# Compressed-branch probabilities transposed in blocks of 32 rows, with high and low parts stacked for one product, and a longer order search

## The chip, the cores and the metric

The kernel runs on one core of one Trainium2 chip. The metric is the time of one execution on the device in microseconds; of several runs the median is given. The engines are named as the profile names them: PE is TensorE (matmuls; PEld is its loading of weights), DVE is VectorE, ACT is ScalarE, POOL is GpSimd, SP is SyncE, which here only issues transfers.

## The reference

One decoder layer over 512 tokens of width 1024, batch 1, in float32. A single RMS norm feeds one input projection, whose columns go to two groups of eight heads of 64:

```
h = rms_norm(x);  proj = h @ w_in
group A:  o = g0 * o_cmp + g1 * o_sel + g2 * o_win      (gates: sigmoids per head)
group B:  per query the 128 keys with the best indexer score, then softmax attention
out = x + concat(A * silu(z_A), B * silu(z_B)) @ w_out
```

The change lies in the compressed branch, `o_cmp`. The keys and values of 32 neighbouring positions, at a stride of 16, are compressed by a small two-layer network to one key and one value, 31 in all (the kernel pads them to 32). Each query attends to the compressed positions that end at or before it:

```
s = q . kc * 64**-0.5;   p = masked_softmax(s, 16*c + 31 <= t);   o_cmp = p @ vc
```

Eight query heads share two groups of keys and values, four heads to a group.

## The kernel before

TensorE multiplies in a rounded float32 format (`fp32r`). To keep precision, nearly every operand is split into a high part, the rounded value, and a low part, the rest; a projection is then three products (high x high, high x low, low x high).

*Stages.* The indexer's columns are projected while the input arrives; then the chunks C (raw compressed keys and values) and B (other keys and values), the indexer's scores and top-128 selection, the hidden layers of the two compressing networks (`hidden`, `hidden1`, `hidden2`, `hidden3`), the queries (chunks Q1, Q2, D), and then attention, woven with the projections D and Z and, from about 226 us, with the output projection.

*Units of attention.* A unit is one query tile of 128 tokens (`i`, 0 to 3), one group (`g`) and one branch. Units of kind "n" are group A: `b` is 0 for the compressed, 1 for the selected, 2 for the window branch. Units of kind "d" are group B. The 512 rows of a tile and group (128 queries x 4 heads) are handled as four blocks of 128 partitions. `softmax_steps` makes the scores, VectorE adds the mask and ScalarE the exponential (`softmax_of`). `transposed` turns the probabilities by TensorE, so that keys lie on partitions and the 512 rows along the free axis, and splits them into `pth` (high) and `ptl` (low). `times_values` multiplies both by the values: the stationary operand holds the values' high part in 64 columns and their low part in 64 more, and the moving operand is 512 columns wide.

*The compressed unit.* A compressed unit has four blocks of 128x32 probabilities, which lie side by side. They are transposed in one go (line 1045), so that block `h` lands on partitions 32h to 32h+31. For one 512-column product each block needs its own columns, so VectorE copies the result four times through a mask, `diag`, which is one only where row block and column block agree (line 1047, tile `pd`); ScalarE copies that to `ph` (line 1049), and GpSimd makes the rest `pl` (line 1050). Two products of 128 rows and 512 columns follow (line 1068). The values must therefore stand four times over on 128 partitions: `hidden1` copies `uT` with `rep = 4`, and `hidden2` loads it as 128 columns of weights (line 816) and writes 128 rows.

*What sets the order.* `set_order` writes the order on every engine, the transfer queue included. It prices every instruction with `cost`, takes the true dependencies and the rings of buffers, and simulates a backward and a forward pass in turn, `ROUNDS` times; the order whose simulated end is earliest is fixed by dependencies between neighbours on an engine. A matmul is priced by its columns and at least 108 ns.

*Other places that the change touches.* `rope` turns queries and keys with two VectorE products into ring buffers (`RTN` of them, lines 539 and 544) and a GpSimd add (line 545). `tables` fills a pair of rotation tables per kind of head. `ARENA` is the size of a shared memory area.

Of the kernel before, what the change touches and what calls it, by code (L numbers as in the profile page):

```python
# [9 lines left out]
F32 = mybir.dt.float32  # L10
F32R = mybir.dt.float32r
BF16 = mybir.dt.bfloat16
I32 = mybir.dt.int32
AF = mybir.ActivationFunctionType
ALU = mybir.AluOpType

S, D, HD = 512, 1024, 64
NT = S // 128
# [41 lines left out]
C_TOT = C_CSIN + HD  # L60


ARENA = 3689 + 272 - 192
ARENA_R = 5376 - 1024

WARM = 10
RTN, RTX = 8, 1
PD = 3

COST = 1 / 2400  # L70
TBUFS, AHEAD, LAG = 2, 2, 2
# [15 lines left out]

URGENT, SOON = 2000, 300
PE_URGENT, PE_SOON = 200, 60
ROUNDS = 8  # L90

FOUR = {"C": range(4), "B": range(4)}

# [16 lines left out]
def set_order(tc):  # L110
# [18 lines left out]
    def cost(i, e):  # L129

        acc = aps(i)
        n = max(free(ap) for _, ap in acc)
        ins = [ap for w, ap in acc if not w]
        bank = any("PSUM" in str(ap.bass_ap.tensor.space) for ap in ins if hasattr(ap.bass_ap.tensor, "space"))
        if "DMA" in type(i).__name__:
            return 450, 128 * n * 4 / 360
        if e == "PE":
            wide = len(ins) > 1 and str(ins[0].dtype).endswith("float32") and not i.is_transpose

            slow = 2 if str(ins[0].dtype).endswith("bfloat16") else 1  # L140
            return max(108, slow * n * (4 if wide else 1) * 0.432 + 10), 0
        if e == "Activation":
            return (50 if bank else 93) + 0.834 * n + 93 * (len(ins) - 1) + 93 * (len(list(i.outs)) - 1), 0
        small = sum(free(ap) == 1 for ap in ins)
        if e == "DVE":
            if "Max" in type(i).__name__ or "MatchReplace" in type(i).__name__:
                return 69 + 1.041 * n + (62 if "Replace" in type(i).__name__ else 0), 0
            return 69 + 61 * small + (0.521 if len(ins) - small < 2 and not bank else 1.041) * n, 0
        return 161 + 83 * small + (0.834 if len(ins) - small < 2 else 2.06) * n, 0
# [27 lines left out]
    for k, i in enumerate(insts):  # L177
        acc = []
        for w, ap in aps(i):
# [4 lines left out]
            end = off + sum((n - 1) * st for st, n in dims[1:] if st > 0) + 1  # L184
# [125 lines left out]
def tile_hybrid_layer(ctx, tc, xT, x, ng, win, gains, peT, w1, b1, w2, wout, cst, out):  # L310
# [19 lines left out]
    def carve(shape, dt):  # L330

        n = 1
        for d in shape:
            n *= d
        w = n // 2 if dt == BF16 else n
        a = arenas[F32R if dt == F32R else F32]
        v = a[0][:, a[1]:a[1] + w]
        a[1] += w
        if dt == BF16:
            v = v.bitcast(dt)  # L340
        if len(shape) == 1:
            return v
        names = "abcde"[:len(shape)]
        return v.rearrange("p (" + " ".join(names) + ") -> p " + " ".join(names), **dict(zip(names[:-1], shape[:-1])))
# [175 lines left out]

    def tables(j, name):
        gn = gns[:, j, None, :]
        tab = work.tile([128, 2, NT, HD], F32, tag=f"tab{j}", name=f"tab{j}", bufs=1)
        c, s = tab[:, 0], tab[:, 1]
        nc.gpsimd.tensor_tensor(c, cosd, gn[:, :, :HD].to_broadcast([128, NT, HD]), op=ALU.mult)
        nc.gpsimd.tensor_tensor(s, sind, gn[:, :, HD:].to_broadcast([128, NT, HD]), op=ALU.mult)
        return c, s
# [203 lines left out]
    kn = [b8.tile([128, 2, 2 * S + 32], F32R, tag=f"kn{g}", name=f"kn{g}") for g in range(2)]  # L731

    K_CMP, K_SEL = S, S + 32
    diag = carve([4, 128], BF16)
    nc.gpsimd.memset(diag, 0.0)
    for h in range(4):
        nc.gpsimd.memset(diag[32 * h:32 * h + 32, h], 1.0)
    w1t = {}
    FSs = {}

# [57 lines left out]
    def hidden1(kv):  # L798
        hid, u = FSs[kv]
        for half in range(2):  # L800
            nc.tensor.transpose(hid[:, 256 + 64 * half:320 + 64 * half], u[:, 128 * half:128 * half + 128], ident[:64, :64])
        src_ = hid[:, 256:384].rearrange("p (a g c) -> p a g c", a=2, g=2)
        rep = 4 if kv else 1
        uT = work.tile([128, 512], F32, tag="uT", name="uT", bufs=1)[:, :128 * rep]
        uT = uT.rearrange("p (a g r c) -> p a g r c", a=2, g=2, r=rep)
        for half in range(2):
            nc.scalar.copy(uT[:, half], src_[:, half, :, None, :].to_broadcast([128, 2, rep, 32]))
        FSs[kv] = (hid, uT)
        yield 0.2

    def hidden2(kv):
        hid, uT = FSs[kv]
        if kv:
            for g in range(2):
                for half in range(2):
                    nc.tensor.matmul(hid[:, 384 + 64 * g:448 + 64 * g], uT[:, half, g].rearrange("p r c -> p (r c)"),
                                     w2t[:, kv, half], start=(half == 0), stop=(half == 1))
        else:
            c2 = hid[:64, 384:448]
            for half in range(2):  # L820
                nc.tensor.matmul(c2, uT[:, half].rearrange("p g r c -> p (g r c)"), w2t[:, kv, half],
                                 start=(half == 0), stop=(half == 1))
        yield 0.4
        if kv == 0:
            kscr = work.tile([128, 512], F32, tag="t2k", name="kscr", bufs=2)[:64]
            sq = kscr[:, 64:128]
            ss = work.tile([64, 1], F32, tag="kss", name="kss", bufs=1)
            y = work.tile([64, 1], F32, tag="ky", name="ky", bufs=1)
            nc.scalar.activation(sq, c2, AF.Square, scale=0.5, accum_out=ss)
            nc.gpsimd.tensor_scalar(ss, ss, 1.0 / HD, EPS, op0=ALU.mult, op1=ALU.add)  # L830
            rsqrt(y, ss, 1, p=64, tag="nk", magic=MAGIC - 2.0 ** 31)
            cg = kscr[:, 128:256].rearrange("p (a b) -> p a b", a=2)
            nc.gpsimd.tensor_tensor(cg[:, 0], ccos, gkc[:64, 0, :HD], op=ALU.mult)
            nc.gpsimd.tensor_tensor(cg[:, 1], csin, gkc[:64, 0, HD:], op=ALU.mult)
            kr = kscr[:, 256:320].rearrange("p (a b) -> p a b", a=1)
            rope(kr, c2, 1, cg[:, 0:1], cg[:, 1:2], p=64, tag="rk", wide=1)
            kr = kscr[:, 256:320]
            nc.gpsimd.tensor_scalar(kr, kr, y[:, 0:1], 0.5, op0=ALU.mult, op1=ALU.mult)
            FSs["kr"] = kr
        else:  # L840
            for g in range(2):
                c2 = hid[:, 384 + 64 * g:448 + 64 * g]
                nc.scalar.activation(vcs[:, g, 0], c2, AF.Copy, scale=0.5)
                nc.vector.scalar_tensor_tensor(vcs[:, g, 1], c2, 0.5, vcs[:, g, 0].bitcast(F32),
                                               op0=ALU.mult, op1=ALU.subtract)

    def hidden3():
# [190 lines left out]
    def transposed(u, item, parts):  # L1038

        p = ps("T", "T_" + u.name)  # L1040
        ph = work.tile([128, 512], F32R, tag="pth", name="pth", bufs=TBUFS)
        pl = work.tile([128, 512], F32R, tag="ptl", name="ptl", bufs=TBUFS)
        if u.b == 0 and u.kind == "n":

            nc.tensor.transpose(p[:, :128], u.P.rearrange("p h c -> p (h c)"), ident)
            pd = work.tile([128, 4, 128], F32, tag="t2k", name="pd", bufs=2)
            nc.vector.tensor_tensor(pd, p[:, None, :128].to_broadcast([128, 4, 128]), diag, op=ALU.mult)
            pd = pd.rearrange("p h q -> p (h q)")
            nc.scalar.copy(ph, pd)
            nc.gpsimd.tensor_tensor(pl, pd, ph.bitcast(F32), op=ALU.subtract)  # L1050
        else:
            blocks = item[0]
            for b, c in blocks:
                nc.tensor.transpose(p[:, b * 128:(b + 1) * 128], u.P[:, b, c:c + 128], ident)  # L1054
            cols = slice(128 * blocks[0][0], 512)
            nc.scalar.copy(ph[:, cols], p[:, cols])  # L1056
            nc.vector.tensor_tensor(pl[:, cols], p[:, cols], ph[:, cols].bitcast(F32), op=ALU.subtract)  # L1057
        parts.append((u, item, ph, pl))

    def times_values(u, item, *parts):  # L1060
        first = u.o[0] is None
        if first:
            u.o[0] = ps("O", "o" + u.name)
        o = u.o[0]
        end = u.last and item is u.items[-1]
        for cols, v in item[1]:
            for x, pp in enumerate(parts):
                nc.tensor.matmul(o[:, cols], v, pp[:, cols], start=(first and x == 0), stop=(end and x == 1))  # L1068
        if end:
            if u.dst is None:  # L1070
                u.dst = work.tile([128, 2, 128], F32, tag="od_" + u.name, name="od_" + u.name, bufs=1)
                od[u.name[1:3]] = u.dst
            combine(o, u.dst)
            u.done()
        return end
# [372 lines left out]
```

## Time and profile before

| what | value |
|---|---|
| median of 3 runs | 308.2 us (308.15 to 308.23) |
| profiled execution, its span | 306.4 us |
| its granted TensorE clock, mean | 0.999 |
| PE busy | 301.3 us, 98% |
| DVE, ACT, POOL busy | 261.0, 240.7, 235.4 us |
| TensorE's share of the chain that ended last | 86% |
| single transposes of compressed units (line 1045) | 8 |

The span runs from the first to the last instruction of the profiled execution; the time of a run is about 1.8 us longer. Matmuls are pipelined: a recorded length holds the way through the array too, so two in a row overlap, and busy shares of TensorE are read with care. Lines are `line engine operation output<-inputs`, then shapes and counts.

### The profile page before, as it was taken

Reading aid. Unit: us, or ns where it says so; the run is one execution under the profiler, and the core shown is the slowest. Engines: PE = TensorE matmul, PEld = TensorE weight load, DVE = VectorE, ACT = ScalarE, POOL = GpSimd, SP = SyncE. Lnnn points to the kernel's source line nnn. Section 1 sums busy time; section 2 is a strip of 40 time slices with the busy share of each in tenths; the row PEclk is TensorE's granted clock in tenths of the full one; section 3 lists DMA queues with packets and bytes.
Section 4 is the critical chain, followed back from the end, with each engine's and each line's share of the span. In section 5 each row is a group of like instructions: output and inputs, shape, how many; then the busy total and the mean of one; then the engine's idle time right before and its main releaser. Section 6 shows DMA issues by size and latency. Waiting matters only on the chain.

```text
span 306.4 us, 5994 instructions
## 1 busy us (share of the span) xinstructions
PE 301.3 (98%) x1669; PEld 256.4 (84%) x1669; DVE 261.0 (85%) x797; ACT 240.7 (79%) x802; POOL 235.4 (77%) x418
## 2 busy tenths in 40 slices
PE   8999999999999999999999999999999999999995
PEld 5997788899878878888888888888888888888885
DVE  4999699999979998998999999999769989986502
ACT  6965776798969999999989999774379998996400
POOL 3099899997996599987989879985667997686410
PEclk9999999999999999999999999999999999999999
DMA  7995345375410034310121023450443343003011
GB/s 282 415 356 181 96 147 163 92 187 158 114 28 0 0 79 125 106 57 3 38 68 39 3 72 106 136 165 0 141 125 120 106 141 103 4 14 122 20 50 68
DMA packets 21249, 32.42 MB, mean 106 GB/s; under 512 B 5664, under 2 KB 8480, under 8 KB 21216
## 3 DMA queue, kind: packets, MB, share of 16 engines
q1 hardware_dynamic: 21216, 32.05, 34.2%
q8 instruction: 13, 0.21, 0.3%
q14 instruction: 20, 0.16, 0.2%
HBM read 29.04 MB, written 2.47 MB: 103 GB/s over the span
## 4 chain that ended last, share of the span: by engine, by line
PE 86%; DVE 4%; ACT 4%; POOL 3%; DMA 2%; issue 1%; DVEq 0%; POOLq 0%
PE out L1268 15%; PE z L401 14%; PE Q L391 8%; PE D L391 7%; PE B L391 7%; PE on L1068 7%; PE s_n L1033 6%; PE T_n L1054 5%; PE od L1068 3%; PE T_d L1054 3%; PE s_d L1033 3%; PE C L401 2%; PE hid L787 2%; ACT hThi L467 2%; POOL wlo_Q L358 2%; PE idx L699 1%
## 5 line engine op out<-in xcount | busy, mean ns | idle before, releaser
L1010 ACT ACTIVATE P_n<-P_n,arena 128x416 f32<-128x416 f32 (+15 forms) x64 | 33.7, 528 | 4.7 <-DVE arena L1003 4.1
L1003 DVE CUSTOM_DVE_ANT_0 P_n<-s_n,arena 128x416 f32<-128x416 f32 (+15 forms) x64 | 31.0, 499 | 1.0 <-PE s_n L1033 0.4
L1023 POOL TENSOR_SCALAR P_n<-P_n,arena 128x416 f32<-128x416 f32 (+15 forms) x64 | 30.8, 501 | 1.2
L1057 DVE TENSOR_TENSOR ptl<-T_n,pth 128x512 fp32r<-128x512 f32 (+1 forms) x40 | 25.0, 627 | 3.6 <-ACT pth L1056 2.9
L1033 PE MATMUL s_n<-kn,arena_r 128*128 128x512 f32 (+11 forms) x104 | 27.1, 342 | 0.0
L710 DVE MAX8 m<-scores 128x8 f32<-128x512 f32 (+2 forms) x48 | 26.5, 552 | 0.6
L401 PE MATMUL z<-hThi,whi_Z 128*128 128x512 f32 x64 | 26.1, 408 | 0.0
L711 DVE MATCH_REPLACE8 scores<-m,scores 128x512 f32<-128x512 f32 (+2 forms) x48 | 26.0, 542 | 0.1
L401 PE MATMUL z<-hTlo,whi_Z 128*128 128x512 f32 x64 | 25.3, 396 | 0.0
L401 PE MATMUL z<-hThi,wlo_Z 128*128 128x512 f32 x64 | 25.2, 397 | 0.0
L1054 PE MATMUL T_n<-arena,P_n 128*128 128x128 f32 x144 | 24.1, 273 | 0.0
L1268 PE MATMUL out<-whi_wo,mx 128*128 128x512 f32 (+1 forms) x72 | 23.8, 374 | 0.0
L1268 PE MATMUL out<-wohi,mx 128*128 128x512 f32 (+1 forms) x72 | 23.7, 377 | 0.0
L1056 ACT CAST pth<-T_n 128x512 fp32r<-128x512 f32 (+1 forms) x40 | 21.5, 540 | 2.7 <-PE od L1068 1.6
L391 PE MATMUL Q<-whi_Q,hThi 128*128 128x256 f32 (+1 forms) x64 | 22.2, 347 | 0.6 <-DVE kn L587 0.6
L391 PE MATMUL Q<-wlo_Q,hThi 128*128 128x256 f32 (+1 forms) x64 | 21.9, 343 | 0.0
L391 PE MATMUL Q<-whi_Q,hTlo 128*128 128x256 f32 (+1 forms) x64 | 21.9, 344 | 0.0
L1054 PEld LDWEIGHTS T_n<-arena,P_n 128*128 128x128 f32 x144 | 18.1, 140 | 4.0
L1033 PEld LDWEIGHTS s_n<-kn,arena_r 128*128 128x128 f32 x104 | 18.1, 189 | 3.3 <-issue 0.2
L358 POOL TENSOR_TENSOR wlo_Z<-raw_Z,whi_Z 128x512 fp32r<-128x512 f32 x16 | 20.4, 1291 | 0.5 <-ACT whi_Z L357 0.5
L358 POOL TENSOR_TENSOR w1l<-raw_w,w1h 128x512 fp32r<-128x512 f32 x16 | 20.4, 1292 | 0.0
L1068 PE MATMUL on<-pth,arena_r 128*128 128x512 f32 (+1 forms) x48 | 18.3, 382 | 0.0
(270 smaller groups left out, 1108.1 us busy)
## 6 DMA issues: line engine op xcount, KB each, us to landing
raw_w<-in_w_dram SPq DMA_DIRECT2D x16, 256.0 KB, 3.7
raw_Z<-in_win_dram SPq DMA_DIRECT2D x16, 256.0 KB, 2.8
wor<-in_wout_dram SPq DMA_DIRECT2D x16, 256.0 KB, 2.8
raw_Q<-in_win_dram SPq DMA_DIRECT2D x12, 256.0 KB, 3.0
raw_D<-in_win_dram SPq DMA_DIRECT2D x8, 256.0 KB, 2.9
xres<-in_x_dram SPq DMA_DIRECT2D x8, 256.0 KB, 3.0
out_dram<-xres SPq DMA_DIRECT2D x7, 256.0 KB, 2.0
xw<-in_xT_dram SPq DMA_DIRECT2D x2, 860.0 KB, 7.8
```

Of the source, the lines that this page charges most:

```text
L358: engine.tensor_tensor(lo, raw, hi.bitcast(F32), op=ALU.subtract)
L391: nc.tensor.matmul(out_ps, a[:, k, tsl], b, start=(k == 0 and b is hi and a is hT["hi"]), stop=(k == KB - 1 and a is hT["lo"]))
L401: nc.tensor.matmul(out_ps, b[:, csl], a[:, k, :], start=(k == 0 and b is hi and a is hT["hi"]), stop=(k == KB - 1 and b is lo))
L710: nc.vector.max(m8, sc)
L711: nc.vector.match_replace(sc, m8, sc, -3e30)
L1003: nc.vector.tensor_tensor_reduce(P, src_, mask, u.r[:, b:b + 1], 3e38, op0=ALU.add, op1=ALU.min, accum_out=m[:, b:b + 1])
L1010: nc.scalar.activation(P, P, AF.Exp, bias=m[:, b:b + 1], scale=-1.0, accum_out=l[:, b:b + 1])
L1023: nc.gpsimd.tensor_scalar(Pb, Pb, l[:, bb:bb + 1], 1.0 if u.gate is not None else 0.5, op0=ALU.mult, op1=ALU.mult)
L1033: nc.tensor.matmul(p, q[0][:, b], k[:, x], start=(x == 0), stop=(x == 1))
L1054: nc.tensor.transpose(p[:, b * 128:(b + 1) * 128], u.P[:, b, c:c + 128], ident)
L1068: nc.tensor.matmul(o[:, cols], v, pp[:, cols], start=(first and x == 0), stop=(end and x == 1))
L1268: nc.tensor.matmul(p, a, b[:, csl], start=(k == 0 and b is hi and a is mx[0]), stop=(k == 7 and a is mx[1]))
```

## The change

In `transposed`, a compressed unit's four blocks are transposed one by one, each into 32 rows and its own 128 columns. ScalarE copies the result to rows 0 to 31 of `ph`, VectorE writes the rest (result minus high part) to rows 32 to 63 of the same tile, and one product with 64 rows replaces two with 128. The mask `diag` and the tile `pl` fall away for these units, and the values stand twice over on 64 partitions (`rep = 2`), once for each part. `times_values` takes a list of products. Beside that, the prices of matmuls in `cost` are rewritten, `ROUNDS` goes from 8 to 20, the rope ring from 8 buffers to 6, two tables share the buffers of two earlier ones, and `ARENA` is 256 words smaller.

```diff
-ARENA = 3689 + 272 - 192
+ARENA = 3689 + 272 - 192 - 256
-RTN, RTX = 8, 1
+RTN, RTX = 6, 1
-ROUNDS = 8
+ROUNDS = 20
...
         if e == "PE":
-            wide = len(ins) > 1 and str(ins[0].dtype).endswith("float32") and not i.is_transpose
-
+            load = 0.845 * free(ins[1])
+            if i.is_transpose:
+                return max(28, load), 0
+            if str(ins[0].dtype).endswith("float32"):
+                return 2 * max(4 + load, 0.864 * n + 10), 0
             slow = 2 if str(ins[0].dtype).endswith("bfloat16") else 1
-            return max(108, slow * n * (4 if wide else 1) * 0.432 + 10), 0
+            return max(load, slow * n * 0.432 + 10), 0
...
-        tab = work.tile([128, 2, NT, HD], F32, tag=f"tab{j}", name=f"tab{j}", bufs=1)
+        tab = work.tile([128, 2, NT, HD], F32, tag=f"tab{j if j < 3 else 5 - j}", name=f"tab{j}", bufs=1)
...
-    diag = carve([4, 128], BF16)
-    nc.gpsimd.memset(diag, 0.0)
-    for h in range(4):
-        nc.gpsimd.memset(diag[32 * h:32 * h + 32, h], 1.0)
...
-        rep = 4 if kv else 1
-        uT = work.tile([128, 512], F32, tag="uT", name="uT", bufs=1)[:, :128 * rep]
+        rep = 2 if kv else 1
+        uT = work.tile([128, 256], F32, tag="uT", name="uT", bufs=1)[:, :128 * rep]
...
-                    nc.tensor.matmul(hid[:, 384 + 64 * g:448 + 64 * g], uT[:, half, g].rearrange("p r c -> p (r c)"),
+                    nc.tensor.matmul(hid[:64, 384 + 64 * g:448 + 64 * g], uT[:, half, g].rearrange("p r c -> p (r c)"),
                                      w2t[:, kv, half], start=(half == 0), stop=(half == 1))
...
-                c2 = hid[:, 384 + 64 * g:448 + 64 * g]
-                nc.scalar.activation(vcs[:, g, 0], c2, AF.Copy, scale=0.5)
-                nc.vector.scalar_tensor_tensor(vcs[:, g, 1], c2, 0.5, vcs[:, g, 0].bitcast(F32),
+                c2 = hid[:64, 384 + 64 * g:448 + 64 * g]
+                nc.scalar.activation(vcs[:64, g, 0], c2, AF.Copy, scale=0.5)
+                nc.vector.scalar_tensor_tensor(vcs[:64, g, 1], c2, 0.5, vcs[:64, g, 0].bitcast(F32),
                                                op0=ALU.mult, op1=ALU.subtract)
...
         ph = work.tile([128, 512], F32R, tag="pth", name="pth", bufs=TBUFS)
+        if u.b == 0 and u.kind == "n":
+
+            for b in range(4):
+                nc.tensor.transpose(p[:32, b * 128:(b + 1) * 128], u.P[:, b], ident)
+            nc.scalar.copy(ph[:32], p[:32])
+            nc.vector.tensor_tensor(ph[32:64], p[:32], ph[:32].bitcast(F32), op=ALU.subtract)
+            parts.append((u, item, [(cols, v[:64], [ph[:64, cols]]) for cols, v in item[1]]))
+            return
         pl = work.tile([128, 512], F32R, tag="ptl", name="ptl", bufs=TBUFS)
-        if u.b == 0 and u.kind == "n":
-
-            nc.tensor.transpose(p[:, :128], u.P.rearrange("p h c -> p (h c)"), ident)
-            pd = work.tile([128, 4, 128], F32, tag="t2k", name="pd", bufs=2)
-            nc.vector.tensor_tensor(pd, p[:, None, :128].to_broadcast([128, 4, 128]), diag, op=ALU.mult)
-            pd = pd.rearrange("p h q -> p (h q)")
-            nc.scalar.copy(ph, pd)
-            nc.gpsimd.tensor_tensor(pl, pd, ph.bitcast(F32), op=ALU.subtract)
...
-        for cols, v in item[1]:
-            for x, pp in enumerate(parts):
-                nc.tensor.matmul(o[:, cols], v, pp[:, cols], start=(first and x == 0), stop=(end and x == 1))
+        for cols, v, moving in products:
+            done = end and (first or v is products[-1][1])
+            for x, pp in enumerate(moving):
+                nc.tensor.matmul(o[:, cols], v, pp, start=(first and x == 0), stop=(done and x == len(moving) - 1))
```

More of the change, by code (lines that the diff above doesn't have):

```diff
@@ L1041, in transposed, with times_values @@
         ph = work.tile([128, 512], F32R, tag="pth", name="pth", bufs=TBUFS)
-        pl = work.tile([128, 512], F32R, tag="ptl", name="ptl", bufs=TBUFS)
-        if u.b == 0 and u.kind == "n":
-            nc.tensor.transpose(p[:, :128], u.P.rearrange("p h c -> p (h c)"), ident)
-            pd = work.tile([128, 4, 128], F32, tag="t2k", name="pd", bufs=2)
-            nc.vector.tensor_tensor(pd, p[:, None, :128].to_broadcast([128, 4, 128]), diag, op=ALU.mult)
-            pd = pd.rearrange("p h q -> p (h q)")
[L1049 to L1060, printed above, removed]
+        if u.b == 0 and u.kind == "n":
[5 more added lines that the diff above has]
+            return
+        pl = work.tile([128, 512], F32R, tag="ptl", name="ptl", bufs=TBUFS)
+        blocks = item[0]
+        for b, c in blocks:
+            nc.tensor.transpose(p[:, b * 128:(b + 1) * 128], u.P[:, b, c:c + 128], ident)
+        cols = slice(128 * blocks[0][0], 512)
+        nc.scalar.copy(ph[:, cols], p[:, cols])
+        nc.vector.tensor_tensor(pl[:, cols], p[:, cols], ph[:, cols].bitcast(F32), op=ALU.subtract)
+        parts.append((u, item, [(cols, v, [ph[:, cols], pl[:, cols]]) for cols, v in item[1]]))
+    def times_values(u, item, products):
         first = u.o[0] is None
```

## The prediction

> **What bounds the kernel now.** I read the page first: its engine shares, its slices and its chain of waits.
>
> ```profile
> span 306.4 us, 5994 instructions
> PE 301.3 (98%) x1669; PEld 256.4 (84%) x1669; DVE 261.0 (85%) x797; ACT 240.7 (79%) x802; POOL 235.4 (77%) x418
> ...
> PE   8999999999999999999999999999999999999995
> ...
> PEclk9999999999999999999999999999999999999999
> ...
> PE 86%; DVE 4%; ACT 4%; POOL 3%; DMA 2%; issue 1%; DVEq 0%; POOLq 0%
> ```
>
> TensorE is busy in every slice, its clock is fully granted, and 86% of the chain is its work. But a matmul's length in the profile holds a pipeline tail, so I checked two more views: the busy time by stretch, and whom TensorE waited for.
>
> ```profile
> 116.00:156.00 40.00, 40.00 (x223) 34.09 (x221) 37.26 (x135) 37.42 (x175) 36.05 (x83) 1.00 0.24 65
> ...
> 226.00:287.00 61.00, 61.00 (x357) 52.27 (x356) 52.27 (x180) 53.73 (x176) 47.17 (x80) 1.00 0.29 90
> ```
> ```profile
> PE I L444 <- DVE arena L446: 1.2, 1, 1.2
> PE Q L391 <- DVE kn L587: 0.6, 1, 0.6
> ```
> ```profile
> PEld on L1068 <- ACT pth L1056: 0.3, 1, 0.3
> ...
> PEld on L1068 <- POOL ptl L1050: 0.2, 1, 0.2
> ```
>
> From 116 to 287 us, where attention runs, the first column after the stretch (its length) and the next (TensorE) are equal. TensorE waits 1.2 us before its first instruction and 0.6 us once near 92 us, and its weight loads wait 0.3 and 0.2 us in front of value products. So the other engines hide behind TensorE, and the change is worth what it takes from or adds to TensorE's own stream, plus what a new order does to these few waits.
>
> **The price of one instruction in that stream** is the distance from one start to the next, not the length.
>
> ```profile
> 134.43 0.40 PE L391 MATMUL D<-wlo_D,hThi 128*128 128x512 f32 x1
> 134.66 0.39 PE L391 MATMUL D<-whi_D,hTlo 128*128 128x512 f32 x1
> 134.89 0.38 PE L621 MATMUL qT_ps<-arena,R_q 128*128 128x128 f32 x2
> 135.11 0.27 PE L1045 MATMUL T_n<-arena 128*128 128x128 f32 x1
> 135.13 0.47 PE L391 MATMUL D<-whi_D,hThi 128*128 128x512 f32 x1
> 135.45 0.39 PE L391 MATMUL D<-wlo_D,hThi 128*128 128x512 f32 x1
> ```
>
> A 512-column product costs 134.66 - 134.43 = 0.23 us. Two transposes take 135.11 - 134.89 = 0.22, 0.11 each. The compressed unit's single transpose (line 1045) and the product after it take 135.45 - 135.11 = 0.34, so it too costs 0.34 - 0.23 = 0.11.
>
> **What sets a transpose's 0.11 us** decides this case. Either it is the load of its weights, the data: then 32 columns in place of 128 make it cheaper. Or it is the stream of the 128 identity columns: then they do not. I look at two places where the loads were not done ahead, and at the same line's first transposes in windows that end one instruction later each time.
>
> ```profile
> 25.51 0.13 PEld L555 LDWEIGHTS rrow_ps<-arena 128*128 128x128 f32 x1 [0.49 <-DVE arena L435]
> 25.51 0.32 PE L555 MATMUL rrow_ps<-arena 128*128 128x128 f32 x1
> ...
> 25.51 0.19 PEld L555 LDWEIGHTS rrow_ps<-arena 128*128 128x128 f32 x2 [0.49 <-DVE arena L435]
> ...
> 25.51 0.30 PEld L555 LDWEIGHTS rrow_ps<-arena 128*128 128x128 f32 x3 [0.49 <-DVE arena L435]
> 25.51 0.43 PE L555 MATMUL rrow_ps<-arena 128*128 128x128 f32 x2
> ```
> ```profile
> L555 PE MATMUL rrow_ps<-arena x4: 270/272/324, 25.5 to 25.9; 128*128 128x128 f32 x4
> ```
> ```profile
> L801 PEld LDWEIGHTS hid<-arena,scr x4: 135/136/139, 69.2 to 110.7; 64*128 64x128 f32 x4
> L801 PE MATMUL hid<-arena,scr x4: 222/247/272, 69.3 to 110.7; 64*128 64x64 f32 x4
> ```
> ```profile
> 69.25 0.20 PEld L801 LDWEIGHTS hid<-arena,scr 64*128 64x128 f32 x2
> ...
> 69.25 0.33 PE L801 MATMUL hid<-arena,scr 64*128 64x64 f32 x2
> ```
>
> The first transpose of line 555 is recorded with its load at 25.51 and is 324 ns long where the others have 272: it waited 0.05 us for 128 columns of weights. The second load begins 0.19 - 0.13 = 0.06 after the first, which says the same; the third only 0.30 - 0.19 = 0.11 later, because it waits for a transpose to stream. So a load of 128 columns takes 0.06 and the transpose 0.11: the load is not what it waits for. Line 801 loads 64x128, its data, and streams 64x64, the identity: the data are the weights, 128 columns of them again, but only 64 identity columns pass. Its second load begins 0.20 - 0.14 = 0.06 after the first; its second transpose ends at 69.58 and is 0.22 long, so it starts 0.05 after the first had its weights. Half the identity columns, half the price. In the change the identity stays 128x128, so I take **0.11 us for each 32-column transpose too**.
>
> No row has a transpose with 32 columns of weights, so both ends stay open. Below: matmuls that are plain float32 do get cheaper with fewer weight columns.
>
> ```profile
> 117.87 1.00 PE L816 MATMUL hid<-arena,uT 128*128 128x64 f32 x8
> ```
> ```profile
> L816 PE MATMUL hid<-arena,uT x8: 218/275/276, 117.9 to 118.6; 128*128 128x64 f32 x8
> ...
> L821 PE MATMUL hid<-arena,uT x4: 220/222/271, 71.1 to 71.4; 128*64 128x64 f32 x4
> ```
> ```profile
> 71.13 0.45 PE L821 MATMUL hid<-arena,uT 128*64 128x64 f32 x4
> ```
>
> Line 816's eight passes load 128 columns each. The first is the short one, 0.22 long, and the last ends 1.00 after its start, so the ends lie (1.00 - 0.22)/7 = 0.11 apart. Line 821's four passes with 64 columns, the first the long one: (0.45 - 0.27)/3 = 0.06. Halved again, 0.03 is the lower end. It is also the distance at which a product is recorded behind a transpose (135.13 - 135.11 = 0.02). Above: if transposes into 32 rows left the quick form, they would run as plain float32, in two passes, 0.22 us each.
>
> **The change part by part.** *Compressed units, eight of them (x8 in line 1045).* Each loses one 512-column product: 8 x 0.23 = 1.84 us off. Each gains three transposes: 24 x 0.11 = 2.64 us on (ends 24 x 0.03 = 0.72; or 32 x 0.22 - 8 x 0.11 = 6.16). The product that stays has half the rows and all 512 columns: no less.
>
> *The value hidden layer (line 816)* loads 64 columns of weights in place of 128, the form of line 821. Seven distances fall from 0.11 to 0.06: 0.35 us off.
>
> *Other engines.*
>
> ```profile
> L1047 DVE TENSOR_TENSOR pd<-T_n,arena x8: 628/686/694, 117.7 to 271.9; 128x512 f32<-128x512 f32 x8
> L1049 ACT CAST pth<-pd x8: 607/622/627, 119.7 to 272.7; 128x512 fp32r<-128x512 f32 x8
> L1050 POOL TENSOR_TENSOR ptl<-pd,pth x8: 1282/1291/1302, 120.7 to 274.2; 128x512 fp32r<-128x512 f32 x8
> ```
> ```profile
> DVE ptl L1057 <- ACT pth L1056: 7.0, 12, 2.0
> ```
> ```profile
> L1057 DVE TENSOR_TENSOR ptl<-T_n,pth x40: 393/684/693, 104.3 to 280.2; 128x512 fp32r<-128x512 f32 x32, 128x256 fp32r<-128x256 f32 x8
> ```
>
> VectorE loses eight masks of 0.69 and gains eight subtractions of the form of line 1057, 0.69 too: nothing. ScalarE keeps its copy. GpSimd loses 8 x 1.29 = 10.3 us, and a unit's way from transpose to product loses that step. The subtraction waits on VectorE for ScalarE's copy, as line 1057 does: 7.0/12 = 0.6 us a wait, so eight more are 4.7 us. Behind it in VectorE's queue stand the masked softmax sums, for which ScalarE's exponentials wait. All of it lies under TensorE, which is full there; were that cover gone, a unit would cost those 0.6. TensorE waited for line 1050 once, 0.2 us: that is the most the shorter way can bring, and I take 0. The mask's memsets and the halved copies of `uT` lie under it as well; were the cover gone, they would be gains.
>
> *Rings and shared tables.* Six rope buffers for eight make a rope's product on VectorE wait for GpSimd's add of six ropes before. A shared table waits for the ropes of chunk B's keys, which end before the later chunks that fill it. Cost 0, with the rival below.
>
> *The order.* New prices and twenty rounds give another order on every engine. A transpose priced at 28 ns moves no wait if it takes 110: copies and everything queued behind it on TensorE slip by the same amount. What an order can give is the 0.6 and 0.5 us of waits above; what it can cost is a wait like the one at 92 us. I take 0.
>
> **Sum:** 2.64 - 1.84 - 0.35 = +0.45 us on the span of 306.4, so 306.8. The runs' median of 308.2 lies 1.8 above that span; with it, **308.6 us**, between 306.4 + 1.8 - 1.5 = 306.7 (0.72 - 1.84 - 0.35 = -1.47) and, with all 32 in the slow form, 312.2 (6.16 - 1.84 - 0.35 = +3.97).
>
> The Trainium skill, TensorE: Matmul & The Clock Gate, section "LDWEIGHTS (loading the stationary operand)", speaks against my step: load time goes with columns, P/1.2, about 107 ns for 128 and 27 for 32, which would make the 0.11 a load. By that and its section "Back-to-back issue gap" (N/2.4 + 2.5, 56 ns for the 128 identity columns) three more transposes are an estimated 0.17 us a unit, and the kernel would take about 307.3. Here the transposing load took 0.06 for 128 columns, and the measurement decides.
>
> **The rivals.**
>
> *Cheap transposes: the load does set the price.* Line 816 against 821 speaks for it, lines 555 and 801 against. 24 x 0.03: **306.7**. Chance 0.19.
>
> *The order recovers the waits.* TensorE's 0.6 us near 92 us and the two in front of value products go: 308.6 - 1.1 = **307.5**. For it: twenty rounds keep the best of more orders by the plan's reckoning, and GpSimd is freer. Against: the stretches after 116 us show TensorE full already. Chance 0.15.
>
> *Slower: the rope ring holds VectorE before the keys.* In the place where TensorE waited for `kn`, VectorE does rope products and GpSimd is far behind with its adds.
>
> ```profile
> 89.97 0.27 DVE L544 TENSOR_TENSOR rt<-Q,tab 128x128 f32<-128x128 f32 x1
> 90.27 0.69 DVE L587 TENSOR_TENSOR kn<-kT_ps,kn 64x512 fp32r<-64x512 f32 x1
> ```
> ```profile
> 88.08 5.02 POOL L358 TENSOR_TENSOR w1l<-raw_w,w1h 128x512 fp32r<-128x512 f32 x4
> 93.07 2.13 POOL L545 TENSOR_TENSOR R_q<-rt,rt 128x256 f32<-128x256 f32 x3
> ```
>
> Three adds stand behind four splits until 93.07. With six buffers the rope at 89.97 would need one of these adds earlier. If the new plan puts one split of 5.02/4 = 1.26 us in front of it, VectorE stands, `kn` behind it comes 1.3 us later, and TensorE, with no slack there, waits: **309.9**. It decides as soon as the add comes after its rope; a plan that moves the add up escapes. Chance 0.18.
>
> *Transposes into 32 rows leave the quick form.* **312.2**. No row speaks for it; line 821's narrower weights did not slow its passes. Chance 0.04. The Trainium skill, TensorEngine Tiling (Array Packing), section "Restrictions", says that column tiling excludes the transpose mode for float32; no row here has a 32-column tile.
>
> **How the numbers follow.** The forecast has 0.44, with its own range of 307.9 to 309.3 (half of a wait like those above, either way). Under 0.2%, about 0.6 us, this kernel's measurement can tell nothing, so no change reaches from 307.6 to 308.8. Faster: 0.18 of the cheap transposes, 0.09 of the better order, 0.03 of the forecast: 0.30. Slower: 0.15 of the forecast, 0.17 of the rope ring, 0.04 of the slow form: 0.36. The rest, 0.34, is no change. The range takes in the cheap end and the rope ring, and leaves the slow form out: 306.6 to 310.2.
>
> **What would show it.** Right: the new transposes start 0.11 us apart, each compressed unit has one 512-column product, line 816's passes lie 0.06 apart, GpSimd's busy time falls by about 10 us with no gain, and TensorE stays full from 116 to 287 us. Distances of 0.03 or 0.06 between the new transposes would make the prediction wrong, and so would a wait over 1 us of TensorE between 60 and 116 us, or none.

## The result, and the profile after

| | before | after |
|---|---|---|
| median | 308.17 us (308.0 to 308.23, 4 runs) | 311.34 us (310.88 to 312.64, 4 runs) |
| ratio, with its 95% interval | 1 | 1.0106 (1.0083 to 1.0129) |
| span of the profiled execution | 306.4 us | 310.9 us (the run of 312.64) |
| GpSimd busy | 235.4 us | 224.6 us |

The changed kernel is 1.1% slower, 3.3 us, and lies outside the predicted range. A second measurement of it on another chip (`changed_again` below) gave 311.31 us and 1.0108. The profiled run is the slowest of the four: TensorE waits 0.5 and 0.4 us in it before 60 us, which it does not in the trace of `changed_again` (a run of 311.19 us), so these waits are not the change's.

The page of the changed kernel, its busy times and its chain of waits:

```profile
PE 305.3 (98%) x1685; PEld 256.3 (82%) x1685; DVE 263.8 (85%) x797; ACT 241.2 (78%) x802; POOL 224.6 (72%) x405
...
PE 89%; ACT 5%; DVE 4%; DMA 1%; issue 0%; ACTq 0%
```

Busy time by stretch (stretch, its length, then busy time and count of PE, PEld, DVE, ACT and POOL, then clock and transfers):

```profile
60.00:116.00 56.00, 56.00 (x347) 48.79 (x346) 52.07 (x157) 49.10 (x190) 49.99 (x99) 1.00 0.39 103
116.00:156.00 40.00, 40.00 (x223) 33.09 (x222) 36.33 (x137) 37.94 (x173) 31.65 (x81) 1.00 0.16 42
...
226.00:287.00 61.00, 61.00 (x353) 51.05 (x352) 52.57 (x178) 52.63 (x170) 43.17 (x76) 1.00 0.29 92
```

GpSimd lost 10.8 us of work, TensorE is full from 60 to 156 us and from 226 to 287 us, and the wait for `kn` near 92 us is gone. By these two views nothing happened to TensorE, yet the kernel lost 3.3 us. The new operations have their own rows: the 32-column transposes (line 1044), and the value products (line 1067) with eight of 64 rows.

```profile
L1044 PEld LDWEIGHTS T_n<-arena x32: 94/96/97, 120.7 to 275.3; 128*32 128x32 f32 x32
L1044 PE MATMUL T_n<-arena x32: 270/272/273, 120.9 to 275.4; 128*32 128x128 f32 x32
```
```profile
L1067 PE MATMUL on<-pth,arena_r x48: 278/395/499, 109.2 to 287.5; 128*128 128x512 f32 x24, 128*128 128x256 f32 x16, 64*128 64x512 f32 x8
```

A transpose is as long as before (272 ns; the start-to-start distance is 0.108 us) although its load fell to 96 ns. The group of the value products says only that eight have 64 rows; its lengths mix many neighbours. So here is one of the eight in the timeline, TensorE first and then its weight loads:

```profile
190.79 0.40 PE L404 MATMUL z<-hTlo,whi_Z 128*128 128x512 f32 x1
191.02 0.40 PE L404 MATMUL z<-hThi,wlo_Z 128*128 128x512 f32 x1
191.35 0.49 PE L1067 MATMUL on<-pth,arena_r 64*128 64x512 f32 x1
191.77 0.50 PE L404 MATMUL z<-hThi,whi_Z 128*128 128x512 f32 x1
192.11 0.40 PE L404 MATMUL z<-hTlo,whi_Z 128*128 128x512 f32 x1
```
```profile
190.79 0.19 PEld L404 LDWEIGHTS z<-hThi,wlo_Z 128*128 128x128 f32 x1
191.35 0.18 PEld L1067 LDWEIGHTS on<-pth,arena_r 64*128 64x128 f32 x1 [0.37 <-issue]
191.77 0.19 PEld L404 LDWEIGHTS z<-hThi,whi_Z 128*128 128x128 f32 x1 [0.24 <-issue]
```

The load for 191.02 starts at 190.79, one product ahead, as loads do in any undisturbed row. The load of the 64-row product does not: it starts at 191.35, when the product before it has streamed its columns and about 0.1 us more has passed (191.35 - 191.02 = 0.33, not 0.23). The load behind it starts only at 191.77, together with its own product. So both loads lie bare on TensorE, with no product running above them. From 190.79 to 192.11 four products take 1.32 us, where four at 0.23 take 0.92: **one 64-row product between 128-row neighbours costs 0.40 us more than a 128-row one**, eight of them 3.2 us. In the list of the weight loads' waits, six of the eight 64-row loads make a row that the kernel before does not have:

```profile
PEld on L1067 <- issue: 1.2, 6, 0.4
```

### The profile page after: what moved, and what is told of

The parts are those of the page before. It is cut to its first block, busy times and chain, and to the rows that moved or that the text cites. A ratio compares the mean times of both kernels' runs of the same rounds, so it can differ in the third digit from the quotient of the medians.

```text
span 310.9 us, 6007 instructions
## 1 busy us (share of the span) xinstructions
PE 305.3 (98%) x1685; PEld 256.3 (82%) x1685; DVE 263.8 (85%) x797; ACT 241.2 (78%) x802; POOL 224.6 (72%) x405
## 4 chain that ended last, share of the span: by engine, by line
PE 89%; ACT 5%; DVE 4%; DMA 1%; issue 0%; ACTq 0%
PE out L1267 15%; PE z L404 13%; PE Q L394 11%; PE D L394 7%; PE B L394 7%; PE on L1067 6%; PE s_n L1032 6%; PE T_n L1052 5%; PE od L1067 3%; PE T_d L1052 3%; PE s_d L1032 3%; PE hid L786 2%; PE C L404 2%; ACT hThi L470 2%; PE qT_ps L624 1%; PE idx L702 1%
## 5 line engine op out<-in xcount | busy, mean ns | idle before, releaser
L1009 ACT ACTIVATE P_n<-P_n,arena 128x128 f32<-128x128 f32 (+14 forms) x64 | 33.6, 527 | 3.1 <-DVE arena L1002 2.7
L1022 POOL TENSOR_SCALAR P_n<-P_n,arena 128x64 f32<-128x64 f32 (+15 forms) x64 | 30.9, 501 | 1.1
L1013 POOL TENSOR_TENSOR arena<-arena 128x4 f32<-128x4 f32 x24 | 4.9, 206 | 20.7 <-DVE arena L1011 20.6
```

Source lines behind the costliest of these rows:

```text
L1009: nc.scalar.activation(P, P, AF.Exp, bias=m[:, b:b + 1], scale=-1.0, accum_out=l[:, b:b + 1])
L1022: nc.gpsimd.tensor_scalar(Pb, Pb, l[:, bb:bb + 1], 1.0 if u.gate is not None else 0.5, op0=ALU.mult, op1=ALU.mult)
```

## The experiments

Ratios are against the kernel before on the same chip, with their 95% intervals.

| run | median, us | ratio |
|---|---|---|
| order_only | 308.27 | 1.0007 (0.9998 to 1.0016) |
| unit_only | 311.7 | 1.0121 (1.0105 to 1.0137) |
| unit_rows128 | 312.08 | 1.0128 (1.0112 to 1.0144) |
| same_order_rows128 | 311.9 | 1.0122 (1.0098 to 1.0146) |
| same_order_rows128_cols128 | 311.53 | 1.0115 (1.0094 to 1.0136) |
| one_transpose_one_product | 310.16 | 1.006 (1.004 to 1.0079) |
| one_transpose_one_product_r20 | 308.64 | 1.0026 (1.0013 to 1.004) |
| changed_again | 311.31 | 1.0108 (1.0092 to 1.0125) |
| same_order_rows128_b | 310.23 | 1.0066 (1.0054 to 1.0078) |
| halves_one_product | 309.95 | 1.0061 (1.0048 to 1.0074) |
| halves_one_product_r20 | 309.62 | 1.0046 (1.0032 to 1.006) |
| changed_shifted | 312.95 | 1.0155 (1.0142 to 1.0168) |
| same_order_rows128_c | 308.76 | 1.0021 (1.001 to 1.0031) |
| halves_one_product_64 | 308.74 | 1.0009 (0.9998 to 1.0021) |
| halves_one_product_64_r20 | 308.79 | 1.0015 (1.0002 to 1.0029) |

My theory after the trace: the unit's 64-row product costs TensorE two breaks. The rivals: the new order has lost something, or the transposes or the narrower hidden-layer passes cost more than they seem.

### The order alone, and the unit alone

`order_only` is the kernel before with the longer search:

```diff
-ROUNDS = 8
+ROUNDS = 20
```

> The kernel before with 20 rounds of the order search and nothing else. Theory S (the 64-row product makes TensorE drain and load its weights uncovered on both sides, some 0.4 us a unit): the order has no part in it, 308.2 +- 0.6 us. Rival O (the new order is what costs the 3.2 us): 310 us or more.

`unit_only` is the changed kernel with the prices and rounds of before:

```diff
-ROUNDS = 20
+ROUNDS = 8
...
-            return max(load, slow * n * 0.432 + 10), 0
+            return max(108, slow * n * (4 if wide else 1) * 0.432 + 10), 0
```

> The changed kernel with the prices of before and 8 rounds of the search; its small rope ring and shared tables stay. S: 308.2 + 24 x 0.11 - 8 x 0.23 (products gone) + 8 x 0.40 (switches) = 312.2 us, no less than 311. O: about 308.6 us, the sum of the prediction.

1.0007 and 1.0121: the longer search alone costs nothing, and the whole loss is there without it and without the new prices. It lies in what `unit_only` keeps: the unit, the hidden layer, the rope ring and the shared tables.

### Whole rows again, with a new order

`unit_rows128` is `unit_only` with the product on 128 rows. GpSimd writes zeros to the upper half, so the sum is the same:

```diff
+    nc.gpsimd.memset(vcs[64:].bitcast(F32), 0.0)
...
+            nc.gpsimd.memset(ph[64:].bitcast(F32), 0.0)
...
-            parts.append((u, item, [(cols, v[:64], [ph[:64, cols]]) for cols, v in item[1]]))
+            parts.append((u, item, [(cols, v, [ph[:, cols]]) for cols, v in item[1]]))
```

> unit_only, but rows 64 to 127 of the high/low tile and of the values are filled with zeros and the single product takes all 128 rows: the same result from the same four transposes, no 64-row product. S: 8 x 0.40 = 3.2 us faster than unit_only, about 309. Rival R (64 rows simply stream at half the rate, 0.42 in place of 0.23 us): 8 x 0.19 = 1.5 us faster than unit_only. O: no change beyond 0.6 us.

Nothing was gained (1.0128 against 1.0121), as the rival O had it and against S. But the planner ordered everything anew, and TensorE has new waits, the two longest of which are:

```profile
PE T_n L1051 <- ACT kdi L588: 0.7, 1, 0.7
PE hid L783 <- POOL w1l L358: 0.5, 1, 0.5
```

The list has 1.4 us of new waits in all, not the whole 3.2; it counts only the part of a wait that no recorded matmul covers, and the rest is not shown. One edit under a planner is two edits. A run that is to price the rows has to keep the order.

### The price by itself

`trains` is the kernel before with rows of products and transposes behind its end that nobody reads (one run):

```diff
+    for _ in range(12):
+        product(0, 128)
+    for _ in range(12):
+        product(0, 64)
+    for _ in range(6):
+        product(0, 128)
+        product(0, 64)
+    for _ in range(6):
+        product(0, 128)
+        product(0, 128, 64)
+    for _ in range(6):
+        product(0, 128)
+        nc.tensor.transpose(pm[:32, :128], src[:, :32], ident)
+    for _ in range(6):
+        product(0, 128)
+        nc.tensor.transpose(pm[:, :128], src[:, :128], ident)
```

> The kernel before with trains of extra matmuls behind its last product, into a bank that nothing reads: 12 products of 128 rows, 12 of 64 rows, 6 pairs of 128 and 64 rows, 6 pairs of 128 columns and 64 columns of weights, 6 pairs of a product and a 32-column transpose, 6 pairs of a product and a 128-column transpose. S: the 64-row train runs at 0.23 us a product like the 128-row one; a 128/64 pair takes 0.23 + 0.63 = 0.86 us. R: the 64-row train at 0.42, a pair 0.65. For the 64-column pairs S has 0.86 too, R 0.46. Both transposes 0.11 us a piece, so 0.34 a pair.

Stretches of the timeline, each a row of `x` products in a train (the form is the first one's): 128 rows, 64 rows, 64 and 128 in turn, then 128 and 64 weight columns in turn. Behind them one 32-column and one 128-column transpose between products.

```profile
303.21 1.98 PE L1361 MATMUL micro<-wohi 128*128 128x512 f32 x8
305.91 2.24 PE L1361 MATMUL micro<-wohi 64*128 64x512 f32 x9
308.73 4.37 PE L1361 MATMUL micro<-wohi 64*128 64x512 f32 x10
314.03 2.46 PE L1361 MATMUL micro<-wohi 128*128 128x512 f32 x10
...
316.59 0.48 PE L1361 MATMUL micro<-wohi 128*128 128x512 f32 x1
316.91 0.27 PE L1375 MATMUL micro<-arena 128*32 128x128 f32 x1
316.94 0.47 PE L1361 MATMUL micro<-wohi 128*128 128x512 f32 x1
...
318.66 0.48 PE L1361 MATMUL micro<-wohi 128*128 128x512 f32 x1
318.97 0.27 PE L1378 MATMUL micro<-arena 128*128 128x128 f32 x1
319.00 0.48 PE L1361 MATMUL micro<-wohi 128*128 128x512 f32 x1
```
```profile
309.59 0.18 PEld L1361 LDWEIGHTS micro<-wohi 64*128 64x128 f32 x1 [0.24 <-issue]
310.02 0.19 PEld L1361 LDWEIGHTS micro<-wohi 128*128 128x128 f32 x1 [0.25 <-issue]
```

A row's length less that of its last product, divided by the number of distances, is (1.98 - 0.39)/7 = 0.23 us for 128 rows, (2.24 - 0.39)/8 = 0.23 for 64 rows, but (4.37 - 0.50)/9 = 0.43 for the two in turn. It is not the 64 rows that cost, it is the change between 64 and 128: **0.20 us each way**, with the load bare at each (0.24 us of idle, then the load). Weight columns in turn cost nothing ((2.46 - 0.40)/9 = 0.23, where my theory had 0.86 for a pair and missed), and a pair of product and transpose takes 316.94 - 316.59 = 0.35 with 32 columns and 319.00 - 318.66 = 0.34 with 128: narrow transposes don't switch.

The Trainium skill, TensorEngine Tiling (Array Packing), section "Key Properties", states that changing the tiling mode, not just the tile, drains TensorE. The runs agree, with 0.20 us a change, if a 64-row product counts as another mode; no trace names the mode.

### Whole rows in the same order

`same_order_rows128` fixes the order of the changed kernel as a list and uses 128 rows. All eight units share one tile whose upper half was zeroed once; that tile is overwritten too early, so some units multiply another unit's probabilities. `same_order_rows128_cols128` also widens the hidden layer's passes to the 128 weight columns of before.

```diff
-    order = best[1]
+    order = {e: [int(x) for x in v.split()] for e, v in FIXED.items()}
...
+    cph = carve([512], F32R)
+    nc.gpsimd.memset(cph[64:].bitcast(F32), 0.0)
```

> The changed kernel with its own order of instructions written in as a list, so that nothing moves; the eight single products take 128 rows, from a tile whose rows 64 to 127 are zeroed once at the start (as are the values' rows), in place of 64. S (a 64-row product costs two switches of 0.20 us): 8 x 0.40 = 3.2 us off the changed kernel's 311.3, so 308.1, and no gap before or behind these products. O (the order and its waits cost the time, as unit_rows128 might be read): no change beyond 0.6 us, 310.7 or more.

> same_order_rows128, and the value hidden layer's eight passes load 128 columns of weights again in place of 64 (values copied four times over), in the same order. The prediction's term: seven distances 0.05 us longer, 0.35 us slower than same_order_rows128. S: the plain float32 passes with 64 columns make TensorE switch as well, in two groups here, so that what the narrower loads save is lost again: no difference beyond 0.3 us, or up to 0.4 faster.

Again no gain: 1.0122 and 1.0115. The shared tile makes a wait of its own (1.6 us of TensorE before scores of line 1040), which the changed kernel doesn't have. `same_order_rows128_b` cures it: the units of the first query tile take a tile of the ring, zeroed by GpSimd, and all units have their own probabilities. `changed_again` ran beside it.

> The changed kernel itself, on the same chip as the next run: 311.3 us, and 311 to 312.6 in single runs, as measured.

> same_order_rows128 mended: there one tile served all eight units, so the compressed unit of query tile 1 lost its probabilities to that of tile 0 and TensorE stood 1.9 us near 157 us. Here the two units of tile 0 have a tile of the common ring, its rows 64 to 127 zeroed by GpSimd each time. Same order, 128 rows, complete result. S: 3.2 us below changed_again, 308 to 308.6. If something other than the 64-row products makes the changed kernel slow: 310 or more.

310.23 against 311.31: 1.1 us gained, a third of the expected 3.2. The breaks were gone, but something else had come.

`same_order_rows128` and `same_order_rows128_cols128` do settle the hidden layer, since their order around it is the same. With 64 columns, and then with 128:

```profile
112.46 0.27 PE L1061 MATMUL T_n<-arena,P_n 128*128 128x128 f32 x1
112.66 0.33 PE L818 MATMUL hid<-arena,uT 128*64 128x64 f32 x2
...
113.28 0.56 PE L818 MATMUL hid<-arena,uT 128*64 128x64 f32 x6
...
113.94 0.38 PE L627 MATMUL qT_ps<-arena,R_q 128*128 128x128 f32 x2
```
```profile
112.83 0.27 PE L1061 MATMUL T_n<-arena,P_n 128*128 128x128 f32 x1
112.94 0.33 PE L818 MATMUL hid<-arena,uT 128*128 128x64 f32 x2
...
113.33 0.78 PE L818 MATMUL hid<-arena,uT 128*128 128x64 f32 x6
...
114.06 0.38 PE L627 MATMUL qT_ps<-arena,R_q 128*128 128x128 f32 x2
```

From the first transpose to line 627 it is 113.94 - 112.46 = 1.48 us with 64 columns and 114.06 - 112.83 = 1.23 with 128. The passes themselves are closer together, as predicted (0.56 for six, not 0.78), but plain float32 passes with 64 columns also switch, in and out, and they stand in two groups: the first starts 0.20 us behind its transpose, not 0.11. Over the whole kernel the two runs differ by less than their intervals.

### Where the missing gain went: addresses

In `same_order_rows128_b` every 512-column product, and not just the units', had a longer distance to the next (the pitch of the forecasts below): 232.0 ns on average, 229.8 in `changed_again` (over the some 700 distances of 200 to 250 ns from one such product to the next matmul in each trace). The two runs with halves below had 232.5 and 232.6. In the built programs these were the ones whose weight tiles (`whi`, `wlo`) do not all start on a multiple of 64 bytes: 39 and 53 of 58 start 32 bytes past one, and none does in the kernels before and after. `changed_shifted` makes that shift alone, in the changed kernel with its order written out (55 of 58 weight tiles are off). It moves nearly everything behind the block: 487 of some 530 other tiles start 32 bytes off too, those of keys and probabilities among them. `same_order_rows128_c` takes the breaks away with every weight tile in place; 229 of its other tiles are off.

```diff
-ARENA = 3689 + 272 - 192 - 256
+ARENA = 3689 + 272 - 192 - 256 - 72
```

> The changed kernel in its own order, written out, with the shared block of constants 72 words shorter (its unused end): nothing is computed otherwise, but every weight tile behind it now starts 32 bytes past a multiple of 64 instead of on one. Theory (the 512-column product's pitch depends on that): pitch 232 to 233 ns instead of 230, about 820 products, so 1.7 to 2.0 us more than the changed kernel, 313.0 to 313.4 us. Rival (the slower pitch of the runs with 128 rows comes from something else in them): pitch 230 and 311.3 us.

```diff
+        m = (k1 - k0) * n
+        xw = wp.tile([128, m + -m % 16], F32, tag=f"xw{k1 - k0}", name=f"xw{k0}", bufs=4 - (k1 - k0))[:, :m]
...
+            nc.gpsimd.memset(ph[64:].bitcast(F32), 0.0)
...
             nc.scalar.copy(ph[:32], p[:32])
```

> Again the changed kernel's own order with 128-row products (rows 64 to 127 zeroed by GpSimd for every unit, in the ring tile itself), now with all weight tiles on multiples of 64 bytes. If the drains at the 64-row products cost 8 x 0.40 = 3.2 us of the path and the 1.8 us missing in the former run were the addresses: pitch 230 and about 308.2 to 308.6 us. If the drains are worth only the 1.1 us that the former run gained: 310.2 us.

The first and the last of 82 products with 512 columns in one unbroken row, in `changed_again`:

```profile
208.83 0.47 PE L404 MATMUL z<-hThi,whi_Z 128*128 128x512 f32 x1
...
227.30 0.39 PE L1067 MATMUL od<-ptl,arena_r 128*128 128x512 f32 x1
```

and the same 82 in `changed_shifted`, whose lines are three further down:

```profile
209.78 0.48 PE L407 MATMUL z<-hThi,whi_Z 128*128 128x512 f32 x1
...
228.72 0.39 PE L1070 MATMUL od<-ptl,arena_r 128*128 128x512 f32 x1
```

(227.30 - 208.83)/81 = 0.2280 us and (228.72 - 209.78)/81 = 0.2338. The shift makes a product 2.5% longer here, over the whole kernel 232.7 ns against 229.8, and the kernel 312.95 us, 1.0155 against 1.0108: 1.5 us (0.8 to 2.1; 1.7 to 2.0 was expected). The rival, that something else in the 128-row runs made their products longer, falls. Which tiles count shows by product, over the same distances. Those that read `whi` or `wlo` stand 229.7 ns apart in `changed_again`, 232.7 in `changed_shifted` and 229.8 in `same_order_rows128_c`, where the weight tiles are back in place. The value products, which read probabilities, have 230.8, 233.0 and 232.5 (each mean uncertain by about 0.5); in `same_order_rows128_c` most tiles of probabilities are still off. So a product seems to follow the start of the tiles that it reads itself.

With the weight tiles in place, `same_order_rows128_c` takes 308.76 us, 0.2 above what was expected. The same place as above, in its trace:

```profile
188.72 0.40 PE L407 MATMUL z<-hTlo,whi_Z 128*128 128x512 f32 x1
188.95 0.39 PE L407 MATMUL z<-hThi,wlo_Z 128*128 128x512 f32 x1
189.18 0.40 PE L1079 MATMUL on<-pth,arena_r 128*128 128x512 f32 x1
189.41 0.40 PE L407 MATMUL z<-hThi,whi_Z 128*128 128x512 f32 x1
189.65 0.40 PE L407 MATMUL z<-hTlo,whi_Z 128*128 128x512 f32 x1
```

Four products take 189.65 - 188.72 = 0.93 us, not 1.32. From 1.0108 to 1.0021 it is 0.87% or 2.7 us (2.1 to 3.3, from both intervals): the eight products' breaks, 3.2 us by the trace. The order is the same in both runs, so it did not cost these 2.7 us. What is left of the change, 0.21% or 0.65 us (0.3 to 0.95), has the size of the predicted sum of 0.45, though not by the predicted terms (see below).

### One transpose and one product

Can the product be saved without the breaks and without the three transposes? `one_transpose_one_product` keeps the single transpose of before; four short ScalarE copies put each 32-row block in its columns, four short VectorE subtractions put the low part into the neighbouring rows, and GpSimd zeroes the rest. One 128-row product follows. It was run with 8 and with 20 rounds.

```diff
+            nc.gpsimd.memset(ph.bitcast(F32), 0.0)
...
+            for h in range(4):
+                at, to = slice(32 * h, 32 * h + 32), slice(32 * (h ^ 1), 32 * (h ^ 1) + 32)
+                cols = slice(128 * h, 128 * h + 128)
+                nc.scalar.copy(ph[at, cols], p[at, :128])
+                nc.vector.tensor_tensor(ph[to, cols], p[at, :128], ph[at, cols].bitcast(F32), op=ALU.subtract)
```

> The kernel before, its order search at 8 rounds and its prices, with another compressed unit: one 128x128 transpose; ScalarE copies each block of 32 rows in place to its own 128 columns of a tile that GpSimd has set to zero; VectorE writes each block's low part to the neighbouring 32 rows, same columns; one product of 128 rows and 512 columns for two, the values standing four times over. Six rope buffers and shared tables for memory. By TensorE's stream: 8 x 0.23 = 1.84 us off, no switch: 306.4 us. If ScalarE's and VectorE's eight short copies a unit in place of two long ones held TensorE, or a new order's waits ate it: 308 or more.

> The same with 20 rounds of the order search. 306.4 us by the stream; 20 rounds can only matter through another order, within 0.6 us of the run with 8.

They took 310.16 and 308.64 us: neither reached 306.4, and they lie 1.5 us apart, not within 0.6. With 20 rounds TensorE waits 0.6 us before a value product for the short VectorE subtractions; the rest of the loss is not separated.

`halves_one_product` keeps VectorE's mask, for two blocks a row half, and GpSimd writes each half's low part into the other half's rows:

```diff
+            for x in range(2):
+                at, to = slice(64 * x, 64 * x + 64), slice(64 - 64 * x, 128 - 64 * x)
+                cols = slice(256 * x, 256 * x + 256)
+                nc.scalar.copy(ph[at, cols], pd[at])
+                nc.gpsimd.tensor_tensor(ph[to, cols], pd[at], ph[at, cols].bitcast(F32), op=ALU.subtract)
```

> The kernel before with its prices, 8 rounds and 8 rope buffers, and another compressed unit: one 128x128 transpose; VectorE masks it into 256 columns in place of 512; ScalarE copies each half of the rows to its own half of 512 columns; GpSimd writes the low parts into the other half of the rows; one product of 128 rows and 512 columns for two. TensorE: 8 x 0.23 = 1.84 us off and no switch, no more work on VectorE, ScalarE 0.1 us a unit: 306.4 us, if the new order has no more waits than that of before. 308 or more if waits of a new order eat it, as in one_transpose_one_product.

> The same with 20 rounds of the order search: 306.4 by the stream, and as far from the run with 8 rounds as two orders differ in their waits (0.6 us).

At 309.95 and 309.62 us both missed 306.4. Of their 58 weight tiles 53 were shifted; the runs `_64` have the shared block 8 words longer and every weight tile in place.

```diff
-ARENA = 3441
+ARENA = 3449
```

> The halves kernel (one transpose and one 128-row product a unit) with the shared block 8 words longer, so that the weight tiles start on multiples of 64 bytes. Address theory: pitch 230 instead of 232.5, 1.7 to 2.0 us off 309.95: 308.0 to 308.3 us. Rival: 309.9 us.

> The same with the 20 rounds of the order search. Address theory: 1.7 to 2.0 us off 309.62: 307.6 to 307.9 us, which would beat the kernel before by some 0.4 us. Rival: 309.6 us.

The addresses gave 0.52% (1.6 us, 1.1 to 2.1) with 8 rounds, about as expected, and 0.31% (1.0 us, 0.4 to 1.5) with 20, half of it; there neither the theory's time nor the rival's came. No version beats the kernel before, though each takes eight products of 0.23 us, 1.84 us, off TensorE. The waits of `halves_one_product_64` show part of where it went:

```profile
PE z L401 <- POOL wlo_Z L358: 0.8, 1, 0.8
PE qT_ps L621 <- POOL R_d L545: 0.2, 1, 0.2
```

TensorE now waits 1.0 us for GpSimd's splits and rope adds, for which it did not wait before. Its wait of 0.6 us near 92 us is gone from this trace, though, and the profiled run is the fastest of its twelve (307.36 us against a median of 308.74). The loss against the hoped-for time is 0.28 + 1.84 = 2.1 us; most of it is not accounted for.

## Why the prediction was wrong

*The step that failed* is the one that had no number: "The product that stays has half the rows and all 512 columns: no less." It was held at 0.23 us. It costs 0.63, because before and after it TensorE changes from 128 to 64 rows and back, at 0.20 us each time. Eight make 3.2 us by the trace and 2.7 by the runs; with the sum of +0.45 that gives 3.1 to 3.7, and 3.3 was measured. The two products that the change replaces cost 0.46 together, so the one that stays is dearer than both.

*The hidden layer* was to save 0.35. The passes did come 0.06 apart, but in the same order the stretch is 0.25 us longer, not shorter: its weights of 64 columns in plain float32 switch too. That is 0.6 us worse than forecast.

*The waits* were taken at nothing, and two of them changed. One left the trace of before (the first two rows), one came into that of the changed kernel:

```profile
91.04 0.28 PE L787 MATMUL hid<-w1h,FS 128*128 128x256 f32 x1
91.95 0.47 PE L391 MATMUL Q<-whi_Q,hThi 128*128 128x512 f32 x1 [0.62 <-DVE kn L587]
```
```profile
167.81 0.49 PE L1067 MATMUL on<-pth,arena_r 128*128 128x512 f32 x1
168.54 0.50 PE L1067 MATMUL on<-ptl,arena_r 128*128 128x512 f32 x1 [0.23 <-DVE ptl L1055]
```

From start to start the first took 91.95 - 91.04 = 0.91 us where a 256-column product takes 0.12, so 0.8 was won. The second took 168.54 - 167.81 = 0.73 where 0.23 is normal, so 0.5 was lost. The rival "the order recovers the waits" came true in this part. With the hidden layer the three come to 0.6 - 0.8 + 0.5 = +0.3 and hide each other in the total. So 0.45 + 0.3 = 0.75 is what the change costs without the 64-row products, by rows; the runs left 0.65 (0.3 to 0.95). That it lies near the predicted 0.45 is in part luck.

*The trace of before showed both breaks*, at 64 rows and at 64 columns, and I had read the rows. Line 801 loads 64 rows and line 821 64 columns, both in plain float32, and I used only the distances inside their groups, not those at their edges:

```profile
70.80 0.28 PE L391 MATMUL Q<-whi_Q,hThi 128*128 128x256 f32 x1
70.92 0.28 PE L391 MATMUL Q<-wlo_Q,hThi 128*128 128x256 f32 x1
71.13 0.45 PE L821 MATMUL hid<-arena,uT 128*64 128x64 f32 x4
71.50 0.39 PE L391 MATMUL Q<-whi_Q,hTlo 128*128 128x256 f32 x1
71.73 0.28 PE L391 MATMUL Q<-whi_Q,hThi 128*128 128x256 f32 x1
```
```profile
PEld hid L801 <- issue: 0.3, 1, 0.3
```

Products of 256 columns stand 0.12 apart; into line 821 it is 71.13 - 70.92 = 0.21, and behind it 71.73 - 71.50 = 0.23. About 0.1 us more at each edge of an odd shape was there to be seen, and to be multiplied by eight.

*What held.* The 32-column transposes cost 0.11, so the disputed term of 2.64 stands, and the rivals of cheap transposes and of the slow form fall: they are 272 ns long, in one pass, and a product behind a narrow one waits no longer than behind a wide one. With the cheap transposes falls the prediction's estimate of 307.3 by the Trainium skill (TensorE: Matmul & The Clock Gate, "LDWEIGHTS (loading the stationary operand)" and "Back-to-back issue gap"). That estimate was also reckoned too high: by the same figures four transposes of 56 ns replace one of 107, an estimated 0.12 us a unit and not 0.17, which makes 307.0. The 312.2 of the slow form came near the measured time by accident; its mechanism did not happen. GpSimd lost 10.8 us, and no gain shows. The longer search gave nothing (1.0007). The rope ring did not hold VectorE: the wait near 92 us went away instead, and "or none" between 60 and 116 us, one of the prediction's own signs of being wrong, came true.

*What my test could not see.* "TensorE stays full from 116 to 287 us" came out nearly true (0.23 us of idle time in the changed kernel's trace) while about 3 us were lost there. A product's recorded length, 0.40 us at a distance of 0.23, covers the breaks of 0.1 and 0.2 us. The distances and the weight loads' waits for "issue" show them; the busy share cannot.

## What to carry to other kernels

Price a matmul by its row and column counts *and those of its neighbours*: one odd shape between 128-row products cost 0.40 us, more than the product itself, while a whole train of the odd shape cost nothing extra; fill it up with zeros, or group the odd ones. In a trace look at the distance into and out of a group and at weight loads that wait for "issue", since a busy share of 100% hides both. When a planner fixes the order, freeze it before comparing variants, and compare the start addresses of the tiles as well.

## What the runs showed of the hardware that was not expected

- Among their like, products of 64 rows run at the pace of 128 (0.23 us for 512 columns); the switch costs 0.20 us each way, as a break of about 0.1 and a load that is not done ahead.
- Which shapes switch among 128-row fp32r products or 128-column transposes: 64 rows in fp32r do (0.43 us a product in turn, not 0.23), and 64 weight columns in plain float32 do (0.21 in front of line 821, not 0.12); 64 weight columns in fp32r (0.23) and transposes with 32 weight columns (0.35 a pair, 0.34 with 128) do not.
- Where the tiles that they read start 32 bytes past a multiple of 64, 512-column products took 1 to 2.5% longer (232.7 ns on average against 229.8, 233.8 against 228.0 in one row of 82), and with nearly all tiles shifted the kernel took 1.5 us longer. Why the address matters no run here shows.
